# Earlier first scores, one more low part on GpSimd and a fixed GpSimd order in the second attention layer of a decoder trunk

## The chip, the cores and the metric

The kernel runs on 1 core of one Trainium2 chip, in one launch. The metric is device microseconds of one execution. The engines are named as the profile names them: PE (TensorE matmul), PEld (its weight load), DVE (VectorE), ACT (ScalarE), POOL (GpSimd), SP (SyncE, which here only issues transfers).

## The reference

The kernel computes a decoder trunk of two layers on 256 tokens of width 1024, all in float32. The part that matters here is the second layer's attention:

```python
N_HEADS, HEAD_DIM, N_KV_HEADS, WINDOW, D_FF = 16, 64, 4, 128, 2816
# layer 0: block-sparse attention with its own q, k, v; then a gated ConvFFN
# layer 1:
hk = rmsnorm(x, kv_norm); k, v = split(hk @ w_kv_b)          # shared K/V, 4 heads
q = partial_rope(heads(rmsnorm(x, attn_norm[1]) @ w_q_b))    # 16 heads
# sliding window of 128, each query head with a learned sink:
logits = q k^T / 8, masked to the band
m = max(max(logits), sink); e = exp(logits - m)
p = e / (sum(e) + exp(sink - m))
x = x + (p v) @ w_o_b
x = x + conv_ffn(rmsnorm(x, ffn_norm[1]))
return rmsnorm(x, final_norm)
```

## The kernel before, in words

**Products.** Each float32 matrix product is made of three matmuls in fp32r: high part by high part, high by low, low by high. So each operand is split: a high part `wh` or `hi` (a rounded copy, made by ACT) and a low part `wl` or `lo` (operand minus high part, made by DVE or POOL). A projection step of `proj` (L345 to L347) is one 128-row chunk of the contraction: three matmuls of 512 columns. A step of `Down.units` (L587 to L590) is six of them.

**Weights.** The weights come in units of 128 x 2048 numbers, in the order of use. `fetch(i)` lets SP issue the transfer of unit i into one of three `raw` buffers; `hi_part` (L181) and `lo_part` (L187 on POOL, L189 or L191 on DVE) make the two parts of a piece, in four `hi` and four `lo` buffers. `prepare(i)` puts a unit's pieces into a chain of steps: high, low, high, low; its last step makes the last low part and then fetches unit i + 3. Here U_QB to U_QB+3 are the q weights of layer 1, U_OB to U_OB+3 its output weights (one unit is two 128-row chunks, the first 1024 numbers and the second 1024), U_UP1 and following the up weights of its FFN. From U_OB+1 on a unit is cut into two pieces of 1024, apart from U_UP1+1 to +3. Before the change POOL makes the low parts of all of U_OB+2 and of the second half of U_OB+3, each 1024 numbers in two instructions of 512; DVE makes all others.

**The order written by the program.** `clock` is a plan's clock, in planned nanoseconds. Whatever is written for PE advances it by `tick`; `chain(key, (delay, step), ...)` puts off a step until the clock has passed its due time (each delay counts from the moment when the step before it was written). `require(key)` writes the pending steps of a key at once. A step of `proj` ticks 640, a step of `Down.units` 1280.

**Layer 1's attention.** There are four groups (g) of four heads, two pairs of heads (j = 2g, 2g + 1) each. `scores(g)` writes the score matmuls (L432 to L434 for the diagonal block of the first 128 queries, L439 for the second 128), `softmax` their chain: masking and row maximum on DVE (L457), exponentials on ACT (L468), a merge of two column blocks on POOL (L463), reciprocal on DVE (L473) and scaling on DVE (L480) and ACT (L478). POOL first writes the sink into the edge columns (L451). `probs_T(j)` transposes a pair's probabilities on PE (L493), which ACT (L502) and DVE (L499) copy; `values(g)` multiplies by v (L538), and ACT (L545) and DVE (L546) split the result o(g). Between these, `fill(ns)` draws steps from a generator until its budget is used up: first the 16 steps of the second half of q, `q_half(1)`, and then 12 steps of the output projection, units U_OB to U_OB+2 (D0 to D11 in the text). What `fill` draws too much is carried over as a negative budget. Ahead of `scores(0)` stands `fill(lead)`. For each half of q, `rotate` copies the projection on ACT (L1013), applies the rotary embedding on DVE (L374 to L380, the rotation), transposes on PE (L386) and splits on ACT (L397) and DVE (L392).

**The order in which engines run.** Within `tc.manual_schedule(engines=...)` an engine keeps the order in which the program wrote its instructions. Outside it, the order on each engine is a list made at compile time, in which an instruction that is ready goes ahead of an earlier one that is not. PE, ACT, DVE and SP are manual up to layer 0's attention (`manual`, closed at L551); in layer 1 only ACT is, from the last group's `values` on (`fixed`, L563, closed in `after_b`, L1044). In both cases each engine runs its list in order.

Of the kernel before, what the change touches and what calls it, by code (L numbers as in the profile page):

```python
# [54 lines left out]
U_OB = U_QB + 4  # L55
# [6 lines left out]
def trunk(ctx: ExitStack, tc, x, xw, pos, cpk, fin, w, out):  # L62
# [34 lines left out]
    def f(ap):  # L97
        return ap.bitcast(F32)
# [4 lines left out]
    def half(n):  # L103
        return slice(n * 512, (n + 1) * 512)
# [34 lines left out]
    def chain(key, *steps, urgent=0):  # L139

        def run(k):
            if urgent:
                with tc.high_priority(offset=urgent):
                    steps[k][1]()
            else:
                steps[k][1]()
            if k + 1 < len(steps):
                put_off.append((clock[0] + steps[k + 1][0], key, lambda: run(k + 1)))
        put_off.append((clock[0] + steps[0][0], key, lambda: run(0)))
# [16 lines left out]
    def fetch(i):  # L166
        if i < N_UNITS:
            raws[i] = wp.tile([P, UNIT], F32, tag="raw", name=f"wr{i}", bufs=3)
            for c in (slice(0, UNIT // 2), slice(UNIT // 2, UNIT)) if 2 <= i < 10 else (slice(0, UNIT),):
                nc.sync.dma_start(raws[i][:, c], w[i][:, c])  # L170

    def gain_of(i, c):

        if not U_KV <= i < U_OB:
            return None
        col = (G_KV + 4 * (i - U_KV) if i < U_QB else G_ATTN1 + 4 * ((i - U_QB) % 2)) + c.start // 512
        return cp[:, col:col + 1]

    def hi_part(i, c):
        g = gain_of(i, c)  # L180
        nc.scalar.activation(wq[i][0][:, c], raws[i][:, c], AF.Copy, **({} if g is None else {"scale": g}))  # L181

    def lo_part(i, c):
        g, raw, hi, lo = gain_of(i, c), raws[i][:, c], f(wq[i][0][:, c]), wq[i][1][:, c]
        if i == U_OB + 2 or i == U_OB + 3 and c.start:
            for h in (half(0), half(1)):
                nc.gpsimd.tensor_tensor(out=lo[:, h], in0=raw[:, h], in1=hi[:, h], op=ALU.subtract)  # L187
        elif g is None:
            nc.vector.tensor_tensor(out=lo, in0=raw, in1=hi, op=ALU.subtract)  # L189
        else:  # L190
            nc.vector.scalar_tensor_tensor(out=lo, in0=raw, scalar=g, in1=hi, op0=ALU.mult, op1=ALU.subtract)  # L191

    def weights(i):
        wq[i] = (spaced(wp, UNIT, F32R, "hi", f"wh{i}", 4),
                 spaced(wp, UNIT, F32R, "lo", f"wl{i}", 4))

    def prepare(i):

        if i >= N_UNITS:
            return  # L200
        n = 4 if i <= 5 or 1 <= i - U_UP0 <= 3 or 1 <= i - U_UP1 <= 3 or U_KV <= i <= U_OB else 2
        cut = [slice(k * UNIT // n, (k + 1) * UNIT // n) for k in range(n)]
        w_time[0] = max(clock[0] + 200.0, w_time[0] + 4500.0, 34000.0 if i == 7 else 0.0)

        def first():
            weights(i)
            hi_part(i, cut[0])

        def last():
            lo_part(i, cut[-1])  # L210
            fetch(i + 3)

        steps = [(w_time[0] - clock[0], first)]
        for k in range(n - 1):
            steps.append((2000.0 / n, lambda k=k: lo_part(i, cut[k])))
            steps.append((2000.0 / n, lambda k=k: hi_part(i, cut[k + 1])))
        chain(("w", i), *steps, (2000.0 / n, last))

    def used(i):

        prepare(i + 4)
# [184 lines left out]
    fixed = ExitStack()  # L406

    def attention(qk, ready, filler, lead, rate, msk, vcol, sink):
# [6 lines left out]
        def fill(ns):  # L415
            budget[0] += ns
            while budget[0] > 0:
                try:
                    budget[0] -= next(filler)
                except StopIteration:  # L420
                    return

        def scores(g):
            while g not in qk:
                next(filler)
            require("qk", g)
            qh, ql, kh_, kl_, kcol, diag = qk[g]
            sd, sa, sb = bank("t" if o_down[0].acc else "acc"), bank("u"), bank("u")
            for p in range(2):
                dh, dl = (t.rearrange("p (e t) -> p t e", e=2) for t in diag(p))  # L430
                o = pairs(sd[:, p * S:(p + 1) * S])
                nc.tensor.matmul(o, ql[:, p, blk(0)], dh, start=True, stop=False)  # L432
                nc.tensor.matmul(o, qh[:, p, blk(0)], dl, start=False, stop=False)
                nc.tensor.matmul(o, qh[:, p, blk(0)], dh, start=False, stop=True)  # L434
            for p in range(2):
                for k, (q_, k_) in enumerate(((ql, kh_), (qh, kl_), (qh, kh_))):
                    for e, o in ((1, sb), (0, sa)):
                        r = slice(e * HD, (e + 1) * HD)
                        nc.tensor.matmul(o[:, p * S:(p + 1) * S], q_[r, p, blk(1)], k_[r, kcol(p)],  # L439
                                         start=(k == 0), stop=(k == 2))  # L440
            tick(1600)
            return [softmax(2 * g + p, p, sd, (sa, sb)) for p in range(2)]
# [106 lines left out]
        ready(oT)  # L549
        fill(lead)  # L550
        manual.close()  # L551
        n_g = NH // 4
        state = scores(0)
        for g in range(n_g):
# [244 lines left out]
    def part(i, c):  # L799
        hi_part(i, c)  # L800
        lo_part(i, c)
# [105 lines left out]
    mask = one.tile([P, S], F32, name="mask")  # L907
# [11 lines left out]
    qk = {}  # L919
# [40 lines left out]
    def ready_a(oT):  # L960
        o_down.append(Down(U_OA, 4, oT, lambda i: require("o", i)))

    attention(qk, ready_a, filler_a(), 9200.0, lambda g: (7000.0, 3500.0, 2000.0) if g < 3 else (4500.0, 2000.0, 1500.0), mask, lambda h: h, False)
    nc.gpsimd.affine_select(out=mask[:, :P], in_=mask[:, :P], compare_op=ALU.is_gt, fill=NEG, base=0,
                            pattern=[[1, P]], channel_multiplier=-1)
# [43 lines left out]
    qk = {}  # L1009
# [5 lines left out]
    def q_half(a):  # L1015
        hi, lo = quad(), quad()
        u = U_QB + 2 * a
        for b in range(NB):
            o = bank("acc")
            yield from proj(o, xT, b, cols512(u), (u, u + 1) if b else ())  # L1020
            rotate(o, 4, b, hi, lo, ("qk", 2 * a), lambda t, b=b, o=o: q_out(t, b, o),
                   wait=750.0 if a or not b else 750.0, turn=2500.0 if a else 1000.0 if not b else 300.0)
        for g in (2 * a, 2 * a + 1):
            c = slice(2 * (g % 2), 2 * (g % 2) + 2)
            qk[g] = (hi[:, c], lo[:, c], kT[:, 0:2], kT[:, 2:4], lambda p, a=a: a, lambda p, a=a: diagonal(0)(a))
# [4 lines left out]
    def filler_b():  # L1030
        yield from q_half(1)
        yield from o_down[0].units(0, 3)

    def ready_b(oT):
        o_down.append(Down(U_OB, 4, oT, lambda i: require("o", i)))

    attention(qk, ready_b, filler_b(), 2100.0, lambda g: (2700.0, 1400.0, 1000.0) if g else (3300.0, 1700.0, 1000.0), mask, lambda h: 2 * (h // 8) + h % 2, True)

    hT = new_hT()
    y = [quad(F32, "y") for _ in range(2)]  # L1040
# [151 lines left out]
```

## Time and profile before

| | |
|---|---|
| Median of 3 runs | 547.96 us (547.95 to 548.14) |
| The profiled execution's own time | 547.73 us |
| Its span | 546.0 us, 9916 instructions |
| PE, PEld busy | 537.8 us (98%), 494.0 us (90%) |
| DVE, ACT, POOL busy | 418.4, 372.2, 132.2 us |
| Granted clock | 0.998 |
| Read from HBM | 99.30 MB, mean 184 GB/s |

Time is in microseconds from the span's start. The stages that the text names: layer 1's k, v and q projections end near 311, its attention lies between 311 and 358, the end of its output projection and the start of the FFN follow, the FFN fills 370 to 520, and the tail ends at 546. A row of the timeline gives start, length, engine, line, operation, tiles and shapes, count, and in brackets the idle time of the engine ahead of it with what ended that time. [...]

### The profile page before, as it was taken

The page shows a single profiled execution, that of the slowest core. Times are in us where ns is not written, and L with a number is a line of the kernel's source. Part 1 is how long each engine was busy: PE and PEld are TensorE (multiplying, and loading weights), DVE is VectorE, ACT ScalarE, POOL GpSimd, SP SyncE. Part 2 cuts the span into 40 slices and gives each one's busy share as a digit, 9 for nine tenths or more (in the row PEclk, how much of TensorE's full clock was granted, in tenths as well). Part 3 has the DMA queues.
Part 4 walks back from the last instruction along what each step waited for, and adds up shares of the span by engine and source line. Part 5 has one row for each costly group of instructions (what it writes and reads, how often), then busy time and mean ns, then how long its engine had stood idle before and what let it go on. Part 6 is the DMA issues. An engine that isn't in the chain of part 4 may idle for free.

```text
span 546.0 us, 9916 instructions
## 1 busy us (share of the span) xinstructions
PE 537.8 (98%) x3742; PEld 494.0 (90%) x3742; DVE 418.4 (77%) x869; ACT 372.2 (68%) x731; POOL 132.2 (24%) x164
## 2 busy tenths in 40 slices
PE   9999999999999999999999999999999999999995
PEld 7888888899999999988888877789999999998884
DVE  6798878689899888864467788889898888884414
ACT  6979777677677777744358798797567777663314
POOL 8422102016223233120001145202332332310003
PEclk9999999999999999999999999999999999999999
DMA  8974445342655665566553534242375656666301
GB/s 317 392 261 175 181 154 185 125 155 79 221 208 200 221 232 206 187 230 226 184 202 144 174 146 155 77 155 88 145 263 201 213 196 214 251 227 215 113 0 77
DMA packets 16464, 100.99 MB, mean 185 GB/s; under 512 B 1952, under 2 KB 2080, under 8 KB 5920
## 3 DMA queue, kind: packets, MB, share of 16 engines
q1 hardware_dynamic: 16128, 100.09, 51.2%
q8 instruction: 29, 0.48, 0.3%
q10 hardware_dynamic: 288, 0.26, 0.1%
q14 instruction: 19, 0.16, 0.1%
HBM read 99.30 MB, written 1.05 MB: 184 GB/s over the span
## 4 chain that ended last, share of the span: by engine, by line
PE 90%; ACT 5%; DVE 3%; issue 1%; DMA 1%; POOL 0%; DVEq 0%; ACTq 0%; POOLq 0%
PE acc L590 8%; PE acc L588 8%; PE acc L587 8%; PE u L681 7%; PE u L682 7%; PE u L680 6%; PE t L681 6%; PE t L682 6%; PE t L680 6%; PE acc L345 5%; PE acc L346 5%; PE acc L347 5%; PE acc L792 2%; PE acc L681 2%; PE acc L682 2%; PE acc L680 2%
## 5 line engine op out<-in xcount | busy, mean ns | idle before, releaser
L189 DVE TENSOR_TENSOR wl<-wr,wh 128x1024 fp32r<-128x1024 f32 (+1 forms) x187 | 204.2, 1112 | 50.3 <-ACT wh L181 49.7
L181 ACT ACTIVATE wh<-wr 128x1024 fp32r<-128x1024 f32 (+1 forms) x190 | 176.7, 958 | 51.4 <-PE acc L590 42.4
L726 POOL TENSOR_TENSOR m<-m,m 128x256 f32<-128x256 f32 x44 | 70.8, 1610 | 166.0 <-DVE m L721 84.2
L587 PE MATMUL acc<-wh,q 128*128 128x512 f32 x238 | 92.2, 387 | 0.2 <-ACT q L545 0.2
L588 PE MATMUL acc<-wl,q 128*128 128x512 f32 x238 | 90.6, 381 | 0.0
L680 PE MATMUL u<-q,wh 128*128 128x256 f32 x320 | 88.3, 277 | 0.0
L681 PE MATMUL u<-q,wh 128*128 128x256 f32 x320 | 88.2, 276 | 0.1
L682 PE MATMUL u<-q,wl 128*128 128x256 f32 x320 | 87.9, 275 | 0.0
L680 PE MATMUL t<-q,wh 128*128 128x256 f32 x288 | 79.2, 275 | 0.0
L681 PE MATMUL t<-q,wh 128*128 128x256 f32 x288 | 79.2, 275 | 0.0
L682 PE MATMUL t<-q,wl 128*128 128x256 f32 x288 | 79.2, 275 | 0.0
L590 PE MATMUL acc<-wh,q 128*128 128x512 f32 x238 | 74.9, 380 | 0.0
L681 PEld LDWEIGHTS u<-q,wh 128*128 128x128 f32 x320 | 61.4, 192 | 0.3 <-DVE q L309 0.3
L682 PEld LDWEIGHTS u<-q,wl 128*128 128x128 f32 x320 | 61.4, 192 | 0.0
L680 PEld LDWEIGHTS u<-q,wh 128*128 128x128 f32 x320 | 61.3, 192 | 0.0
L680 PEld LDWEIGHTS t<-q,wh 128*128 128x128 f32 x288 | 55.3, 192 | 0.0
L681 PEld LDWEIGHTS t<-q,wh 128*128 128x128 f32 x288 | 55.3, 192 | 0.0
L682 PEld LDWEIGHTS t<-q,wl 128*128 128x128 f32 x288 | 55.3, 192 | 0.0
L587 PEld LDWEIGHTS acc<-wh,q 128*128 128x128 f32 x238 | 45.0, 189 | 7.0 <-ACT q L545 0.6
L590 PEld LDWEIGHTS acc<-wh,q 128*128 128x128 f32 x238 | 44.8, 190 | 6.2 <-issue 0.2
L588 PEld LDWEIGHTS acc<-wl,q 128*128 128x128 f32 x238 | 45.1, 189 | 5.8 <-issue 0.2
L345 PE MATMUL acc<-wh,q 128*128 128x512 f32 x128 | 50.2, 392 | 0.0
(182 smaller groups left out, 1008.5 us busy)
## 6 DMA issues: line engine op xcount, KB each, us to landing
wr<-in_w SPq DMA_DIRECT2D x82, 1024.0 KB, 4.8
wr<-in_w SPq DMA_DIRECT2D x16, 512.0 KB, 6.5
first<-in_xw SPq DMA_DIRECT2D x7, 384.0 KB, 6.4
xr<-in_x SPq DMA_DIRECT2D x2, 512.0 KB, 8.3
fin_t<-in_fin SPq DMA_DIRECT2D x1, 512.0 KB, 5.6
out<-ot SPq DMA_DIRECT2D x1, 512.0 KB, 2.6
first<-in_xw SPq DMA_DIRECT2D x1, 388.0 KB, 3.5
out<-m ACTq DMA_DIRECT2D x1, 256.0 KB, 2.1
```

The costliest lines, as they stand in the source:

```text
L181: nc.scalar.activation(wq[i][0][:, c], raws[i][:, c], AF.Copy, **({} if g is None else {"scale": g}))
L189: nc.vector.tensor_tensor(out=lo, in0=raw, in1=hi, op=ALU.subtract)
L345: nc.tensor.matmul(o, xh[:, blk(b)], wh, start=(c == 0), stop=False)
L346: nc.tensor.matmul(o, xh[:, blk(b)], wl, start=False, stop=False)
L347: nc.tensor.matmul(o, xl[:, blk(b)], wh, start=False, stop=(c == KC - 1))
L587: nc.tensor.matmul(o, ph[:, blk(b)], turns(hi[:, s_]), start=first, stop=False)
L588: nc.tensor.matmul(o, ph[:, blk(b)], turns(lo[:, s_]), start=False, stop=False)
L590: nc.tensor.matmul(o, pl[:, blk(b)], turns(hi[:, s_]), start=False, stop=end)
L680: nc.tensor.matmul(o, hi[:, s_], xh, start=(c == 0), stop=False)
L681: nc.tensor.matmul(o, hi[:, s_], xl, start=False, stop=False)
L682: nc.tensor.matmul(o, lo[:, s_], xh, start=False, stop=(c == KC - 1))
L726: nc.gpsimd.tensor_tensor(out=h, in0=gs, in1=t[1], op=ALU.mult)
```

## The change

It has four parts. The `lead` of layer 1's attention is 1500 instead of 2100. The second half of unit U_OB+1 has its low part made by POOL instead of DVE. The delay of a unit's last step (last low part and fetch) is set for three units: 300 for U_OB+1, 2500 for U_OB+2 and U_OB+3, where it was 1000. From the first scores of layer 1 until `after_b`, POOL is manual too. The diff, whole:

```diff
     def lo_part(i, c):
         g, raw, hi, lo = gain_of(i, c), raws[i][:, c], f(wq[i][0][:, c]), wq[i][1][:, c]
-        if i == U_OB + 2 or i == U_OB + 3 and c.start:
+        if i == U_OB + 2 or i in (U_OB + 1, U_OB + 3) and c.start:
             for h in (half(0), half(1)):
                 nc.gpsimd.tensor_tensor(out=lo[:, h], in0=raw[:, h], in1=hi[:, h], op=ALU.subtract)
         elif g is None:
@@
         for k in range(n - 1):
             steps.append((2000.0 / n, lambda k=k: lo_part(i, cut[k])))
             steps.append((2000.0 / n, lambda k=k: hi_part(i, cut[k + 1])))
-        chain(("w", i), *steps, (2000.0 / n, last))
+        late = {U_OB + 1: 300.0, U_OB + 2: 2500.0, U_OB + 3: 2500.0}.get(i, 2000.0 / n)
+        chain(("w", i), *steps, (late, last))
@@
         ready(oT)
         fill(lead)
         manual.close()
+        if sink:
+            fixed.enter_context(tc.manual_schedule(engines={mybir.EngineType.Pool}))
         n_g = NH // 4
         state = scores(0)
@@
-    attention(qk, ready_b, filler_b(), 2100.0, lambda g: ..., mask, ..., True)
+    attention(qk, ready_b, filler_b(), 1500.0, lambda g: ..., mask, ..., True)
```

`sink` is true only for layer 1.

More of the change, by code (lines that the diff above doesn't have):

```diff
@@ L1035, in ready_b @@
         o_down.append(Down(U_OB, 4, oT, lambda i: require("o", i)))
-    attention(qk, ready_b, filler_b(), 2100.0, lambda g: (2700.0, 1400.0, 1000.0) if g else (3300.0, 1700.0, 1000.0), mask, lambda h: 2 * (h // 8) + h % 2, True)
+    attention(qk, ready_b, filler_b(), 1500.0, lambda g: (2700.0, 1400.0, 1000.0) if g else (3300.0, 1700.0, 1000.0), mask, lambda h: 2 * (h // 8) + h % 2, True)
     hT = new_hT()
```

## The prediction

> **What bounds the kernel now.** I read the page's first part, then the busy time by stage, then PE's timeline through layer 1's attention, and last what ACT, DVE and POOL did ahead of each hole.
>
> ```profile
> PE 537.8 (98%) x3742; PEld 494.0 (90%) x3742; DVE 418.4 (77%) x869; ACT 372.2 (68%) x731; POOL 132.2 (24%) x164
> ```
>
> PE is the bound almost everywhere. The stages (columns: us, then each engine's busy time and instructions, clock, DMA):
>
> ```profile
> 370.00:520.00 150.00, 150.00 (x1185) 145.38 (x1184) 118.00 (x183) 97.24 (x152) 35.52 (x23) 1.00 0.56 194
> 520.00:546.00 26.00, 19.92 (x99) 17.42 (x97) 8.06 (x19) 7.47 (x17) 4.37 (x4) 0.96 0.10 40
> ```
>
> ```profile
> 308.00:323.00 15.00, 14.83 (x86) 12.32 (x85) 12.60 (x41) 13.20 (x33) 2.39 (x7) 1.00 0.46 176
> 323.00:345.00 22.00, 21.72 (x150) 17.15 (x148) 19.04 (x65) 19.03 (x56) 13.08 (x19) 1.00 0.27 96
> 345.00:358.00 13.00, 12.78 (x88) 10.05 (x88) 9.58 (x34) 9.05 (x30) 2.02 (x4) 1.00 0.23 83
> ```
>
> The second FFN (370 to 520) leaves PE no idle time, and the change ends before it. Layer 1's attention, 308 to 358, shows 0.17 + 0.28 + 0.22 us idle. A matmul's shown length overlaps the next one's, so the holes are larger than that; I take them from starts. The change can win only there, or lose there.
>
> ```profile
> 315.35 0.38 PE L345 MATMUL acc<-wh,q 128*128 128x512 f32 x1
> 315.90 0.98 PE L439 MATMUL u<-q,q 64*128 64x256 f32 x12 [0.17 <-DVE q L392]
> ...
> 323.58 0.28 PE L434 MATMUL acc<-kd,q 128*128 128x256 f32 x1
> 323.78 0.97 PE L439 MATMUL u<-q,q 64*128 64x256 f32 x12
> ...
> 330.09 0.46 PE L587 MATMUL acc<-wh,q 128*128 128x512 f32 x1
> 330.39 0.38 PE L588 MATMUL acc<-wl,q 128*128 128x512 f32 x1
> 330.61 0.38 PE L587 MATMUL acc<-wh,q 128*128 128x512 f32 x1
> 330.82 0.38 PE L588 MATMUL acc<-wl,q 128*128 128x512 f32 x1
> 331.30 0.62 PE L493 MATMUL u<-ident,m 128*128 128x128 f32 x3
> 331.68 0.68 PE L590 MATMUL acc<-wh,q 128*128 128x512 f32 x2
> ...
> 338.48 0.70 PE L590 MATMUL acc<-wh,q 128*128 128x512 f32 x2
> 339.36 0.48 PE L587 MATMUL acc<-wh,q 128*128 128x512 f32 x1 [0.18 <-ACT q L545]
> ...
> 341.73 0.49 PE L493 MATMUL u<-ident,m 128*128 128x128 f32 x3
> 341.98 0.68 PE L590 MATMUL acc<-wh,q 128*128 128x512 f32 x2
> ...
> 350.11 0.46 PE L587 MATMUL acc<-wh,q 128*128 128x512 f32 x1
> 350.79 0.62 PE L493 MATMUL u<-ident,m 128*128 128x128 f32 x3 [0.22 <-ACT m L478]
> 351.16 0.46 PE L588 MATMUL acc<-wl,q 128*128 128x512 f32 x1
> ```
>
> A 512-column product takes 0.215 us of PE (330.61 to 330.82), so a `proj` step of three is 0.65 and a `Down` step of six 1.29. The holes:
> - S1, first scores: 315.57 to 315.90, 0.33; a change to 64-row tiles costs 0.09 anyway (323.58 + 0.11 to 323.78), so about 0.23.
> - S2, transposes of pair 2: 331.04 to 331.30, 0.26, and three of them take 0.38 against 0.25 at 341.73: 0.39.
> - S3, `Down` unit 1 waits for o(1): the second L590 began at 338.80 (its end, 339.18, less 0.38), so 339.02 to 339.36: 0.34.
> - S4, transposes of pair 6: 0.68 from 350.11, where 0.30 is usual after a transpose (330.09 to 330.39): 0.38, and 0.37 against 0.25: 0.50.
>
> Together 1.46 us, all that can be won but crumbs of 0.1.
>
> **The change part by part.**
>
> *Lead 2100 to 1500.* A step costs 640 on the plan's clock: 2100 is used up after 4 steps (-460 left), 1500 after 3 (-420). The next budgets, 3300, 1700 and 1000, still draw 5, 3 and 1, so scores 0 stand behind 3 steps instead of 4 and scores 1 behind 12 instead of 13. Nothing is removed; three products go behind. What fed the scores before:
>
> ```profile
> 311.79 2.00 ACT L181 ACTIVATE wh<-wr 128x1024 fp32r<-128x1024 f32 x2
> 314.23 0.61 ACT L397 ACTIVATE q<-t 128x512 fp32r<-128x512 f32 x1 [0.44 <-PE t L386]
> ```
>
> ```profile
> 312.52 0.29 DVE L380 TENSOR_TENSOR m<-rb 128x128 f32<-128x128 f32 x1
> 312.88 2.36 DVE L189 TENSOR_TENSOR wl<-wr,wh 128x1024 fp32r<-128x1024 f32 x2
> 315.16 0.68 DVE L392 TENSOR_TENSOR q<-t,q 128x512 fp32r<-128x512 f32 x1
> ```
>
> ```profile
> 313.59 0.60 PE L386 MATMUL t<-ident,m 128*128 128x128 f32 x4
> ```
>
> The rotation ended at 312.81 and PE turned q only at 313.59, behind twelve products. With nine it can at 312.94, 0.65 earlier. ACT is in L181 to 313.79, so L397 runs 313.79 to 314.40, not 314.23 to 314.84.
>
> *The low part of U_OB+1.* L392 waited for DVE's second L189, whose end is about 315.24. That instruction (half of 2.36, 1.18 us) leaves DVE: free at about 314.06, it starts L392 at 314.40 and ends at 315.08, and L439 can begin 0.75 us earlier. The program emits the two parts of the scores (L434, L439) together, yet the trace has a product of L345 right ahead of L439: PE's order here is a compiled list order that puts in what is ready. I take all of S1, 0.23; bounds: 0 if the order keeps the old distance, 0.33 with the shape change too. POOL pays, by these rows (and has time, idle 16.50 us):
>
> ```profile
> 318.59 0.88 POOL L463 TENSOR_TENSOR m<-m 128x128 f32<-128x128 f32 x2 [16.50 <-ACT m L468]
> ...
> 323.83 5.03 POOL L187 TENSOR_TENSOR wl<-wr,wh 128x512 fp32r<-128x512 f32 x4 [0.61 <-ACT wh L181]
> ```
>
> Two of L187 are 2 x 1.26 = 2.52 us, 314.0 to 316.5, and merges begin near 318: nothing on the path. SP's fetch of U_UP1 waits for it, some 1.3 us later than 315.24; ACT takes up those weights only at 339.70:
>
> ```profile
> 339.70 1.04 ACT L181 ACTIVATE wh<-wr 128x1024 fp32r<-128x1024 f32 x1
> ```
>
> So more than 20 us cover it; without that cover it would cost its 1.3.
>
> *`late` and the given order on POOL.* On the plan's clock, from the end of the first q half: U_OB+1 is due at 1700 and written at 1920; its first low part (due 2920) is written at 3960, after the scores' tick of 1600, its second high part (due 4960) at 5240, so the last step is due at 5540 (with 1000: 6240). The first exponentials are written at 5240 too, their merge due 600 later, 5840. So POOL's order is: four L451, the pair for U_OB+1, the four merges of group 0, four L451, the first pair of U_OB+2, the merges of group 1 (three due at 15480, the fourth 16760), the second pair (due 18020), L451 for group 2, the pair of U_OB+3, merges. Before, all four L187 of U_OB+2 stood in one block ahead of group 1's merges, which came late:
>
> ```profile
> 326.99 0.51 ACT L468 ACTIVATE m<-m,hst 128x257 f32<-128x257 f32 x1
> ```
>
> ```profile
> 328.79 1.72 POOL L463 TENSOR_TENSOR m<-m 128x128 f32<-128x128 f32 x4
> ...
> 341.31 1.01 POOL L463 TENSOR_TENSOR m<-m 128x128 f32<-128x128 f32 x1 [0.98 <-ACT m L468]
> ```
>
> An exponential of group 1 that a merge needs ended at 327.50, and POOL came at 328.79. With only one pair ahead (323.8 to 326.4) that 1.3 us goes, more than S2's 0.39: I take all of it; bounds 0 (norms late for ACT's sake) to 0.39. The fetch of U_UP1+1 goes behind the second pair, to about 331.5 instead of 328.9: 8 us ahead of even U_UP1's use, which comes before its own. That of U_UP1+2 keeps its place behind the pair of U_OB+3.
>
> *Later fills.* A `Down` step costs 1280. Before, 2700 drew the last three q steps and D0 ahead of pair 2, then came D1, pair 3, D2, scores 2, D3 and D4, pair 4, D5, pair 5, D6, scores 3. Now 2700 draws the last four q steps (-40 left), 1400 draws D0 and D1 (-1200), 1000 draws none, and so on: pair 2, D0, D1, pair 3, scores 2, D2, D3, pair 4, D4, D5, pair 5, scores 3. So D2 and D3 stand behind values(1), 1.29 us more between it and D4, which must wait for o(1): S3's 0.34 goes (bounds 0, 0.34). Scores 2 lose D2 as a cover; D1 before them and D2, values(1) and D3 behind can be drawn ahead, at no cost if the list order does it. S4 gets nothing directly: two steps stand between values(2) and pair 6 as before. I leave it (bounds 0, 0.50, if its scores get DVE sooner).
>
> The tail (520 to 546) has 6 us without PE, but runs the same instructions after 150 us of full PE: no change there. Sum: 0.23 + 0.39 + 0.34 = 0.96 us. The profiled execution took 547.73 (span 546.0 and 1.7 around it), so 546.8; the median stands 0.23 above it, so 547.0.
>
> **The rivals.** *All four holes close* (S4 too): -1.46, 546.5. For it: scores 3 come right behind pair 5, so DVE's masking may start earlier. Against: S4 ends by ACT's L478, and ACT loses no work.
>
> *The second pair of U_OB+2 collides with the rotation* (slower). It now follows group 1's merges, near 329, where DVE rotates q's second half:
>
> ```profile
> 340.77 1.23 DVE L189 TENSOR_TENSOR wl<-wr,wh 128x1024 fp32r<-128x1024 f32 x1
> ```
>
> ```profile
> 330.52 0.28 DVE L374 TENSOR_TENSOR rb<-m,cs 128x128 f32<-128x128 f32 x1
> ...
> 331.10 0.29 DVE L380 TENSOR_TENSOR m<-rb 128x128 f32<-128x128 f32 x1
> ```
>
> The merge at 341.31 took 1.01 us, 0.5 over the pair's 0.44 each at 318.59, and ended 0.32 after this L189: POOL waited for DVE. If DVE waits likewise, L187 can hold the rotation up to 2 x 1.26 = 2.5 us, and through it L386, L397, L392 and scores 2. It decides once the pair starts before L380 ends. Less a cover of up to D2's 1.29 it costs 1.2, on PE's fixed order 2.5; S2 and S3 would not pay for it: 547.96 - 0.23 + 1.2 to 2.5 = 548.9 to 550.2. Against: the masking, which reads PSUM and one SBUF tile, took 0.48 us outside the block of L187 and inside it:
>
> ```profile
> 317.32 0.48 DVE L457 CUSTOM_DVE_ANT_0 m<-u,mask,nsink 128x256 f32<-128x256 f32 x1
> ...
> 325.31 0.48 DVE L457 CUSTOM_DVE_ANT_0 m<-u,mask,nsink 128x256 f32<-128x256 f32 x1
> ```
>
> The rotation reads SBUF twice, though, as L189 does.
>
> [...]
>
> *Little moves*: the list order had already put products where they fit, and gives holes back elsewhere; 0 to -0.5, 547.7.
>
> **How the numbers follow.** Forecast (-0.5 to -1.1) 0.38; all holes (beyond -1.1) 0.34; little (within 0.5 either way) 0.16; collision 0.12, 0.11 of it beyond +1.1. 0.2% is 1.1 us, about what a measurement can tell. So faster 0.34, same 0.55, slower 0.11. Range 546.1 (all 1.46 and 0.4 of crumbs) to 549.0 (lower end of the collision); the forecast's own is 546.8 to 547.5.
>
> **What would show it.** Right: L386 near 312.9 and L439 near 315.1 with no hole; two L187 ahead of POOL's first merge; merges of group 1 from about 326.5; no wait of L587 on L545 after values(1); the first L680 of FFN 1 about 1 us earlier. Wrong: a stretched L374 or L480 beside L187, a wait of L439 on L392 at scores 2, or holes that only move behind 339.

## The result and the profile after

The kernel became slower: 552.73 us (median of 5 runs, 552.36 to 553.03) against 547.99 (547.95 to 548.34), a ratio of 1.0083 (95% interval 1.0072 to 1.0094). The prediction was 547.0, with a range of 546.1 to 549.0: the time lies above the range, and on the other side of the kernel before. The profiled execution took 552.73 us, of which the span is 551.0.

The page's first part shows almost nothing: the same 3742 products, and 2.4 us more of "busy" on PE. The last line of the fence, out of the page's second part, does show something. Each figure there is a slice of 13.8 us, and the 25th (331 to 344) has a granted clock below 0.9:

```profile
span 551.0 us, 9935 instructions
...
PE 540.2 (98%) x3742; PEld 495.9 (90%) x3742; DVE 420.3 (76%) x868; ACT 372.7 (68%) x731; POOL 132.2 (24%) x166
...
PEclk9999999999999999999999998999999999999999
```

Busy time by stage of the changed kernel (columns as before: PE, PEld, DVE, ACT, POOL, clock, DMA):

```profile
308.00:323.00 15.00, 14.96 (x88) 12.27 (x88) 12.05 (x40) 13.20 (x34) 4.83 (x10) 1.00 0.52 187
323.00:345.00 22.00, 18.90 (x123) 14.36 (x123) 17.65 (x56) 15.42 (x49) 12.03 (x17) 0.92 0.27 96
...
375.00:525.00 150.00, 150.00 (x1185) 145.38 (x1184) 118.03 (x184) 97.09 (x152) 35.49 (x23) 1.00 0.54 194
```

The loss is in one stretch, 323 to 345: PE is without work for 3.10 us there, where it was 0.28, and runs at a clock of 0.92. The waits of PE between 308 and 372 (what waited, for what, total, times, longest) name the place:

```profile
PE t L387 <- DVE m L381: 2.9, 1, 2.9
PE t L539 <- DVE pT L500: 0.3, 1, 0.3
PE u L494 <- ACT m L479: 0.2, 1, 0.2
```

L387 is the transpose of q's second half (L386 before; the code has moved down by a line there), and L381 the last instruction of the rotation (L380 before). PE's timeline of the changed kernel, first at the scores 0 and at pair 2, then around L387:

```profile
315.23 0.38 PE L346 MATMUL acc<-wh,q 128*128 128x512 f32 x1
315.55 0.97 PE L440 MATMUL u<-q,q 64*128 64x256 f32 x12
...
329.14 0.46 PE L590 MATMUL acc<-wh,q 128*128 128x512 f32 x1
329.80 0.62 PE L494 MATMUL u<-ident,m 128*128 128x128 f32 x3 [0.19 <-ACT m L479]
...
333.53 0.38 PE L590 MATMUL acc<-wh,q 128*128 128x512 f32 x1
333.75 0.38 PE L591 MATMUL acc<-wl,q 128*128 128x512 f32 x1
337.03 0.66 PE L387 MATMUL t<-ident,m 128*128 128x128 f32 x4 [2.91 <-DVE m L381]
337.63 0.58 PE L433 MATMUL t<-kd,q 128*128 128x256 f32 x1
...
339.93 0.63 PE L590 MATMUL acc<-wh,q 128*128 128x512 f32 x1
340.36 0.63 PE L591 MATMUL acc<-wl,q 128*128 128x512 f32 x1
...
341.88 1.52 PE L539 MATMUL t<-pT,v 128*64 128x256 f32 x16
```

Read two things. From L591 to L387 there is a hole: 337.03 less 333.965 (333.75 and 0.215 of pace) is 3.06 us. And behind it two successive products of 512 columns stand 0.43 apart (339.93 to 340.36), twice the 0.215 of 333.53 to 333.75. PE runs there at half its pace.

What DVE did meanwhile, and what POOL did:

```profile
331.32 2.21 DVE L189 TENSOR_TENSOR wl<-wr,wh 128x1024 fp32r<-128x1024 f32 x1 [1.25 <-ACT wh L181]
333.46 0.68 DVE L500 TENSOR_TENSOR pT<-u,v 128x512 f32<-128x512 f32 x1
334.06 1.25 DVE L375 TENSOR_TENSOR rb<-m,cs 128x128 f32<-128x128 f32 x1
335.24 1.42 DVE L380 TENSOR_TENSOR rb<-m,sn 128x64 f32<-128x64 f32 x2
336.69 0.29 DVE L381 TENSOR_TENSOR m<-rb 128x128 f32<-128x128 f32 x1
```

```profile
314.42 2.56 POOL L187 TENSOR_TENSOR wl<-wr,wh 128x512 fp32r<-128x512 f32 x2 [11.84 <-ACT wh L181]
...
326.80 0.95 POOL L464 TENSOR_TENSOR m<-m 128x128 f32<-128x128 f32 x2 [0.16 <-ACT m L469]
...
329.94 2.51 POOL L187 TENSOR_TENSOR wl<-wr,wh 128x512 fp32r<-128x512 f32 x2
332.40 1.55 POOL L452 COPY m<-nsink 128x2 f32<-128x2 f32 x4
333.91 2.52 POOL L187 TENSOR_TENSOR wl<-wr,wh 128x512 fp32r<-128x512 f32 x2
```

From 331.32 to 336.98 DVE shows no idle time, only instructions that have become long. One half low part, L189, takes 2.21 us instead of 1.22; the first rotation instruction 1.25 instead of 0.28; the next two 1.42 instead of 0.35. That is 0.99 + 0.97 + 1.07 = 3.03 us more. Each long one is let go about where one of POOL's L187 ends. The pair at 329.94 (second half of U_OB+2) ends at 332.45, and L189 ends 1.08 us behind that, within its usual 1.22; the two of the pair at 333.91 (U_OB+3) end at 335.17 and 336.43, where L375 and L380 are released.

In the kernel before, the order on DVE was another. The rotation stood ahead of L189, and PE came to the transposes later than the rotation was done:

```profile
331.31 1.22 DVE L189 TENSOR_TENSOR wl<-wr,wh 128x1024 fp32r<-128x1024 f32 x1
332.44 0.68 DVE L499 TENSOR_TENSOR pT<-u,v 128x512 f32<-128x512 f32 x1
```

```profile
333.93 0.60 PE L386 MATMUL t<-ident,m 128*128 128x128 f32 x4
```

Its rotation (quoted in the prediction) ended at 331.39, so it had 2.54 us to spare before PE asked at 333.93. In the changed kernel L189 and L500 are listed ahead of it, and nothing is left to spare. ACT's list changed likewise: the copy of the projection, which the rotation reads, stood ahead of ACT's high part (L181, 329.90) in the kernel before and stands behind it (L181, 330.23) in the changed one. The row of before, then that of the changed kernel:

```profile
329.33 0.67 ACT L1013 ACTIVATE m<-acc,rstd 128x512 f32<-128x512 f32 x1
```

```profile
331.18 0.68 ACT L1016 ACTIVATE m<-acc,rstd 128x512 f32<-128x512 f32 x1
```

So the rotation could not have begun before 331.86, wherever DVE had it. The chain of the changed kernel (start, length, what) shows the whole path, from the weights on ACT to the matmuls that run slow:

```profile
330.33 0.97 ACT wh L181
...
331.32 2.21 DVE wl L189
...
335.31 1.35 DVE rb L380 x2
...
337.03 0.66 PE t L387 x4
```

Before any experiment this makes one theory: two pairs of POOL's L187 meet DVE's low part and rotation (3 us), and PE's clock falls after so long a hole (the rest). The rivals: the given order on POOL itself costs (small work waits behind large), or the new list order costs, with the L187 as bystanders. The expectations below call the first half of the theory "port", after a guess of the author's (two readers of SBUF take turns); no trace shows a port, only how long the instructions took.

### The profile page after: what moved, and what is told of

Read it like the earlier page. It is cut to its first block, busy times and chain, and to the rows that moved or that the text cites. A ratio compares the mean times of both kernels' runs of the same rounds, so it can differ in the third digit from the quotient of the medians.

```text
span 551.0 us, 9935 instructions
## 1 busy us (share of the span) xinstructions
PE 540.2 (98%) x3742; PEld 495.9 (90%) x3742; DVE 420.3 (76%) x868; ACT 372.7 (68%) x731; POOL 132.2 (24%) x166
## 3 DMA queue, kind: packets, MB, share of 16 engines
HBM read 99.30 MB, written 1.05 MB: 182 GB/s over the span
## 4 chain that ended last, share of the span: by engine, by line
PE 90%; DVE 4%; ACT 3%; issue 1%; DMA 1%; DVEq 0%; ACTq 0%
PE acc L593 8%; PE acc L591 8%; PE acc L590 8%; PE u L684 7%; PE u L685 6%; PE u L683 6%; PE t L685 6%; PE t L683 6%; PE t L684 6%; PE acc L346 5%; PE acc L347 5%; PE acc L348 5%; PE acc L795 2%; PE acc L684 2%; PE acc L685 2%; PE acc L683 2%
## 5 line engine op out<-in xcount | busy, mean ns | idle before, releaser
L189 DVE TENSOR_TENSOR wl<-wr,wh 128x1024 fp32r<-128x1024 f32 (+1 forms) x186 | 203.3, 1113 | 50.9 <-ACT wh L181 50.6
L181 ACT ACTIVATE wh<-wr 128x1024 fp32r<-128x1024 f32 (+1 forms) x190 | 176.3, 956 | 50.9 <-PE acc L593 42.2
L729 POOL TENSOR_TENSOR m<-m,m 128x256 f32<-128x256 f32 x44 | 69.2, 1573 | 167.7 <-DVE m L724 97.9
L591 PE MATMUL acc<-wl,q 128*128 128x512 f32 x238 | 91.0, 382 | 0.0
L591 PEld LDWEIGHTS acc<-wl,q 128*128 128x128 f32 x238 | 45.2, 190 | 6.1 <-issue 0.3
```

The costliest lines, as they stand in the source:

```text
L591: nc.tensor.matmul(o, ph[:, blk(b)], turns(lo[:, s_]), start=False, stop=False)
L729: nc.gpsimd.tensor_tensor(out=h, in0=gs, in1=t[1], op=ALU.mult)
```

## The experiments

Each ratio is against runs of the kernel before on the same chip. One measure from the traces stands beside it: the distance from ACT's second copy of q's first half (L1013 before, L1016 in the changed kernel), just ahead of what the change touches, to the first product of the FFN, just behind:

| kernel | copy, first product | distance | against before | ratio (95%) |
|---|---|---|---|---|
| before | 311.20, 363.69 | 52.49 | | |
| after | 311.69, 368.70 | 57.01 | +4.52 | 1.0083 (1.0072 to 1.0094) |
| a_lead | 311.15, 364.74 | 53.59 | +1.10 | 1.002 (1.001 to 1.003) |
| b_order | 311.16, 365.50 | 54.34 | +1.85 | 1.0034 (1.0021 to 1.0047) |
| c_no_order | 311.34, 364.88 | 53.54 | +1.05 | 1.0017 (1.0008 to 1.0027) |
| e_writes | 311.17, 363.63 | 52.46 | -0.03 | 1.0002 (0.9992 to 1.0011) |
| m_first | 311.68, 365.05 | 53.37 | +0.88 | 1.0023 (1.0013 to 1.0034) |
| n_second | 311.47, 364.88 | 53.41 | +0.92 | 1.0013 (1.0004 to 1.0023) |
| f_fill | 311.66, 368.37 | 56.71 | +4.22 | 1.0084 (1.007 to 1.0098) |
| k_part | 311.91, 363.94 | 52.03 | -0.46 | 0.9994 (0.9985 to 1.0002) |
| p_lead2100 | 311.48, 366.05 | 54.57 | +2.08 | 1.0031 (1.0019 to 1.0044) |
| s_b_edges | 311.50, 364.16 | 52.66 | +0.17 | 1.0003 (0.9993 to 1.0012) |
| q_edges | 311.43, 364.61 | 53.18 | +0.69 | 1.001 (1.0001 to 1.0019) |
| r_edges_late | 311.71, 364.16 | 52.45 | -0.04 | 0.9997 (0.9988 to 1.0006) |

In the changed kernel all stands 0.49 us later already at that copy, ahead of the change. The copies of the other kernels scatter as far, from 311.15 to 311.91, and why was not tried. It is in the 552.73, and not in the 4.52.

**The lead alone** (the kernel before, with one number changed):

```diff
-    attention(qk, ready_b, filler_b(), 2100.0, ...
+    attention(qk, ready_b, filler_b(), 1500.0, ...
```

> Only the lead is changed (1500 for 2100); POOL's order and its low parts are as before. PE's and DVE's lists are then nearly those of the changed kernel: on DVE the rotation of q's second half stands behind a low part (L189) and a copy (L499) instead of ahead of them. Theory (port): the pair of L187 for U_OB+3 starts near 333.4 and meets the rotation, which waits for one or both: a hole of PE of 1 to 2 us ahead of scores 2, 549 to 551. Rival (lost cover: `Down` step D2 no longer stands ahead of scores 2): the hole comes from PE's list, so it is as large as in the changed kernel, 552 to 553, with DVE's instructions at their usual lengths.

Slower by 1.10 us on the table's measure. The wait of PE, the only large one, and the DVE row behind it, both from this kernel:

```profile
PE t L386 <- DVE m L380: 0.8, 1, 0.8
```

```profile
333.67 1.24 DVE L380 TENSOR_TENSOR m<-rb 128x128 f32<-128x128 f32 x1
```

The shorter lead alone already puts the rotation so late in DVE's list that its last instruction meets the pair of U_OB+3 on POOL, and takes 1.24 us instead of 0.29. The "lead" is no tuning of the front: it renumbers everything behind.

**The given order on POOL alone** (the kernel before, with the added `manual_schedule`):

```diff
+        if sink:
+            fixed.enter_context(tc.manual_schedule(engines={mybir.EngineType.Pool}))
```

> Only POOL's given order; lead, low parts and late steps as before. PE's and DVE's lists are word for word those of before, and POOL's has the four L187 of U_OB+2 ahead of group 1's merges as before. Theory (port): 547.7 to 548.3. Rival (a given order on POOL costs by itself, because it waits in line): over 549.

Slower by 1.85 us, where the theory expected next to nothing; the rival is right for this kernel. The mechanism is another one. The first row is POOL's, the last one ACT's:

```profile
323.78 2.53 POOL L187 TENSOR_TENSOR wl<-wr,wh 128x512 fp32r<-128x512 f32 x2 [1.73 <-ACT wh L181]
326.24 0.56 POOL L451 COPY m<-nsink 128x2 f32<-128x2 f32 x4
```

```profile
326.47 0.41 ACT L468 ACTIVATE m<-m,hst 128x129 f32<-128x129 f32 x1 [1.54 <-POOL m L451]
```

Group 1's four edge copies, 0.56 us in all, are written behind the first pair, and ACT's exponentials wait for the edge columns. With the old lead this holds; with the new one the edges of group 1 come out ahead of that pair (in the changed kernel L452 runs at 320.70, L187 at 324.11), so this cost is not in the 4.52.

**The changed kernel without the given order:**

```diff
-        if sink:
-            fixed.enter_context(tc.manual_schedule(engines={mybir.EngineType.Pool}))
```

> The changed kernel without POOL's given order. PE's and DVE's lists are word for word those of the changed kernel; on POOL all four L187 of U_OB+2 stand ahead of group 1's merges again, so only the pair of U_OB+3 can meet the rotation. Theory (port): L189 beside it falls from 2.21 to 1.2 us, the rotation meets one or two L187 instead of queueing behind three, a hole of 1 to 2 us, 549 to 551. Rival (PE's list, lost cover): unchanged, 552 to 553.

1.05 us instead of 4.52. PE and DVE run the same lists as in the changed kernel; only POOL's order differs, and with it one meeting is left, that of the pair of U_OB+3 with the rotation's last instruction:

```profile
331.22 1.23 DVE L189 TENSOR_TENSOR wl<-wr,wh 128x1024 fp32r<-128x1024 f32 x1 [1.34 <-ACT wh L181]
...
333.55 1.25 DVE L381 TENSOR_TENSOR m<-rb 128x128 f32<-128x128 f32 x1
```

So the lists of PE and DVE by themselves do not cost the 4.5. What they cost with no L187 beside the rotation, the next run shows.

**The two pairs without their reading.** POOL's second pair of U_OB+2 and the pair of U_OB+3 become writes (two `memset` of the same tile, 1.97 us instead of 2.51). Those low parts are left out of the output. The lists of PE and DVE stay those of the changed kernel.

```diff
+            if i > U_OB + 1 and c.start:
+                for _ in range(2):
+                    nc.gpsimd.memset(f(lo), 0.0)
+                return
```

> The changed kernel with the last two pairs of L187 (second half of U_OB+2, U_OB+3) replaced on POOL by memsets of the same tiles, two for each half: POOL stays busy at the same places of its list but reads no SBUF; the low parts of these halves are left out (zero). PE's and DVE's lists are unchanged. Theory (port: two readers of SBUF take turns): L189, L375 and L380 go back to 1.2, 0.3 and 0.35 us, the rotation ends near 334, the hole of 3.1 us and the low clock behind it vanish: 546.5 to 548. Rival 1 (PE's list): 552 to 553. Rival 2 (DVE waits for POOL by order, not for its port): as long as the memsets are busy, 550 to 552.

The loss is gone: -0.03 us. POOL still works all through the rotation, as its row and then DVE's show (lines are 5 further down here):

```profile
332.39 1.96 POOL L189 MEMSET wl<- 128x1024 f32 x2
```

```profile
329.19 1.27 DVE L486 TENSOR_SCALAR m<-m,hst 128x128 f32<-128x128 f32 x1
...
332.56 0.28 DVE L380 TENSOR_TENSOR rb<-m,cs 128x128 f32<-128x128 f32 x1
332.75 0.35 DVE L385 TENSOR_TENSOR rb<-m,sn 128x64 f32<-128x64 f32 x2
333.14 0.29 DVE L386 TENSOR_TENSOR m<-rb 128x128 f32<-128x128 f32 x1
```

So here it is POOL's reading of SBUF (of two inputs; one was not tried) that holds these two-input instructions of DVE, not POOL's being busy: beside reads the first took 1.25 us and the next two 1.42, beside writes 0.28 and 0.35. The rotation ends at 333.43 and PE takes up the transposes at 333.49, without a hole: the changed order leaves the rotation no slack (0.06 us, against 2.54 before), but costs nothing by itself. And with the collisions gone nothing is gained either; that is the other half of the wrong forecast.

**One pair at a time.** m_first replaces only the second pair of U_OB+2, n_second only the pair of U_OB+3 (low parts left out likewise).

```diff
+            if i == U_OB + 2 and c.start:      # n_second: i == U_OB + 3
+                for _ in range(2):
+                    nc.gpsimd.memset(f(lo), 0.0)
+                return
```

> The changed kernel with only the second pair of U_OB+2 as memsets (that low part is left out, zero); the pair of U_OB+3 stays. PE's and DVE's lists unchanged. Theory (port, and a clock that falls only after a long hole): L189 back to 1.2 us, L381 or one L380 still waits for an L187, a hole near 1 us as without the given order, no low clock: 548.8 to 549.6.

> The changed kernel with only the pair of U_OB+3 as memsets (left out, zero); the second pair of U_OB+2 stays. Theory: L189 takes 2.2 us, the rotation its usual 0.3 and ends near 335, a hole near 1 us, clock 1.00: 548.8 to 549.8. So the two pairs alone cost about 1 each, together 4.5, the difference being the second wait in a row and the low clock. Rival (costs add up without a clock effect): the two alone sum to 4.5, one of them at least 2.2 above before, over 550.4.

Either pair alone costs 0.9 us (0.88, 0.92). PE's row of m_first, then that of n_second:

```profile
334.95 0.66 PE L391 MATMUL t<-ident,m 128*128 128x128 f32 x4 [0.82 <-DVE m L385]
```

```profile
334.77 0.66 PE L391 MATMUL t<-ident,m 128*128 128x128 f32 x4 [0.87 <-DVE m L385]
```

Together they cost 4.5, not 1.8. First, with the first pair alive, the rotation begins 1 us later, and the second pair takes two of its instructions instead of one: three waits, 3.03 us. Second, the clock. From the transposes to values(1), the same list of instructions took 4.85 us in the changed kernel (337.03 to 341.88) and 3.24 in m_first (334.95 to 338.19), 3.24 in n_second, 3.23 in e_writes: 1.61 us more. A window of 3.4 us behind the hole in the changed kernel, and the same window in m_first:

```profile
337.60:341.00 3.40, 3.40 (x13) 2.54 (x12) 1.87 (x9) 1.71 (x7) 0.00 (x0) 0.51 0.74 294
```

```profile
337.60:341.00 3.40, 3.40 (x34) 2.42 (x31) 3.15 (x16) 3.40 (x16) 0.87 (x2) 1.00 0.72 299
```

A hole of 1.0 us, 0.82 of it shown as idle, leaves the clock at 1.00; one of 3.06 us, 2.91 shown idle, is followed by a clock of 0.51 for 3.4 us. 3.06 + 1.61 = 4.67. The whole distance to e_writes, which has neither, is 4.55 (57.01 less 52.46), so these two terms account for it to within 0.12 us.

**The hole filled with other work.** To keep PE busy and see the clock stay, pair 3's transposes run seven times over (24 more of them, the output unchanged).

```diff
-                    nc.tensor.transpose(tp[:, e, k], ...
+                    for _ in range(7 if j == 3 else 1):
+                        nc.tensor.transpose(tp[:, e, k], ...
```

> The changed kernel with the eight-fold... transposes of pair 3 written seven times (24 more transposes, 2.6 us more work for PE, same results) so that PE is busy in most of the hole ahead of scores 2. Theory (the hole of 3.1 us itself brings the clock down to a half for 3 us): the granted clock stays at 1.00 behind it, and although PE does 2.6 us more, the time falls by about 1.5 us to 551.0 to 551.6. Rival (the low clock has another cause): clock low all the same, 552.5 or more.

```profile
332.63 3.22 PE L495 MATMUL t<-ident,m 128*128 128x128 f32 x28
337.02 0.66 PE L387 MATMUL t<-ident,m 128*128 128x128 f32 x4 [1.17 <-DVE m L381]
```

```profile
337.00:341.00 4.00, 3.98 (x38) 3.41 (x40) 2.90 (x13) 1.78 (x8) 0.00 (x0) 1.00 0.74 266
```

The hole stood at the same place, its idle part cut to 1.17 us, and the clock stayed at 1.00. The time did not fall with it (+4.22), because the compiled list put other products elsewhere. Counted from the copy of the table, values(1) begins 1.81 us earlier than in the changed kernel (340.04 and 341.88 on the two clocks), but with four products of 512 columns (0.86 us) fewer done ahead of it, and pairs 4 and 6 then wait anew (0.44 and 0.15 us shown idle). So it agrees with a clock that falls with PE's own idleness, as POOL and DVE met here as before; but that the time falls with the hole, as was expected, it did not show. The 1.61 us of clock rest on the comparison with m_first, n_second and e_writes.

**U_OB+1's low part alone** (the kernel before, with `lo_part`'s new condition only):

```diff
-        if i == U_OB + 2 or i == U_OB + 3 and c.start:
+        if i == U_OB + 2 or i in (U_OB + 1, U_OB + 3) and c.start:
```

> The kernel before with only the low part of U_OB+1's second half on POOL; lead, late steps and POOL's order as before. DVE's list keeps the rotation of q's second half ahead of L189, so no L187 meets it. Theory: L392 of the first scores no longer waits for L189, S1 shrinks by about 0.2 us, the rest as before: 547.5 to 548.0, at best a little faster. Rival (any more work on POOL costs): 548.5 or more.

547.54 against 548.11, ratio 0.9994 (0.9985 to 1.0002): at best half a microsecond, not told from none. Of all kernels it alone has a distance shorter by more than a tenth of a microsecond.

**The old lead, all else as changed**, and three kernels around the edge copies. p_lead2100 is the changed kernel with a lead of 2100. In s_b_edges (from b_order), q_edges (from p_lead2100) and r_edges_late (from q_edges) the edge copies are written ahead of the scores; r_edges_late also gives U_OB+2 and U_OB+3 their old delay.

```diff
         # s_b_edges, q_edges, r_edges_late: in scores(g), ahead of its tick
+            pre = [edges(2 * g + p) for p in range(2)] if sink else [None] * 2
         # r_edges_late
-        late = {U_OB + 1: 300.0, U_OB + 2: 2500.0, U_OB + 3: 2500.0}.get(i, 2000.0 / n)
+        late = {U_OB + 1: 300.0}.get(i, 2000.0 / n)
```

> The changed kernel with the lead back at 2100 (given order on POOL, low part of U_OB+1 and late steps stay). PE's and DVE's lists are then those of before but for U_OB+1: the rotation stands ahead of L189 and ends about 2.5 us before PE wants it. On POOL the edge copies of group 1 (L452) now stand behind the first pair of U_OB+2, as in the run with the given order alone, and the second pair ahead of group 1's fourth merge. Theory (the lead took the slack that would hide a collision; edges behind a pair cost 1 to 2 us by themselves): no hole ahead of the transposes of q, clock 1.00, 549 to 550.5. Rival (the collision costs the same with any lead): 552 or more.

> The given order on POOL alone, but the edge copies are written ahead of the scores' tick, so that group 1's stand ahead of the first pair of U_OB+2. PE's and DVE's lists as before. Theory (the given order cost 1.8 us because the exponentials of group 1 waited for edges queued behind a pair of L187): back to 547.8 to 548.5. Rival (merges or other things behind one another in the given order): still 549 or more.

> The changed kernel with the lead at 2100 and the edge copies written ahead of the scores' tick. Only the second pair of U_OB+2 (behind three merges of group 1) and that of U_OB+3 can now hurt. Theory: the second pair meets the rotation near 330 to 331 or L189, but 2.5 us of slack hide it; the fourth merge waits for the pair, so pair 3's transposes come late: 547.3 to 549. Rival: the collision costs its 2 to 3 us again, 550 or more.

> As the last one, with the late steps of U_OB+2 and U_OB+3 back at 1000: on POOL all four L187 of U_OB+2 stand ahead of group 1's merges as before, the edges ahead of them. Of the change there are left the low part of U_OB+1 on POOL (late 300) and the given order. Theory: the same as with the low part alone, 547.3 to 548.0, which is as fast as or a little faster than before. Rival (a given order costs something in itself): 548.5 or more.

p_lead2100 costs 2.08: the lead cannot be the sole cause. Here the edges wait behind the first pair as in b_order, and the second pair, at 330.55, meets the norm instead of the rotation (DVE's row):

```profile
330.40 2.73 DVE L481 TENSOR_SCALAR m<-m,hst 128x128 f32<-128x128 f32 x3
```

Three of these take 0.68 in b_order (330.54), with one merge on POOL beside their start, and 1.28 in the kernel before (328.90), beside POOL's merges all along. s_b_edges brings b_order's 1.85 down to 0.17, so the edges behind the pair were its cause. q_edges, with the edges early, still pays 0.69, with the same long norm (2.75 us). r_edges_late, whose second pair keeps the old delay, costs nothing (-0.04). A given order on POOL is free here, then, when the small work that others wait for goes first, and the large work is due where DVE has nothing urgent. It gains nothing either: no version here beats the kernel before beyond its interval.

## Why the prediction was wrong, by its steps

- **S1 was right, and small.** L440 begins at 315.55 with about 0.1 of hole; from q's copy it is 3.86 us against 4.70, of which 0.65 is the moved step and 0.19 gained (0.23 predicted). The pair for U_OB+1 runs at 314.42, ahead of the first merge, as said.
- **S2 was wrong.** Group 1's merges did come earlier (326.80 instead of 328.79), but pair 2's transposes still waited, for ACT's share of the norm: 0.19 idle before them at 329.80, the last line of the waits above. The chain of the kernel before had run there too: ACT's copy (329.33), its L181 (329.90) and its share of the norm (330.85) stand ahead of the transposes at 331.30, and no merge does. The term took all of the bound where its own lower end, "norms late for ACT's sake", was the truth.
- **S3 went, S4 went, and both came back.** No `Down` product waits for L546 any more, but values(2) now waits for a copy of the probabilities (L539 on L500, 0.3 in the waits above). In e_writes, with no collision, this wait and pair 2's remain, and the distance is that of before. The forecast of -0.96 added up holes; the list order made others. That was the rival "little moves", at a chance of 0.16.
- **"D1 before them and D2, values(1) and D3 behind can be drawn ahead, at no cost if the list order does it"** is the step that failed. It looked at what PE's list could draw ahead and not at what the lists of the engines that feed it would do. On ACT the rotation's input went behind L181, on DVE the rotation went behind L189 and L500, and its slack fell from 2.54 us to 0.06. The shorter lead alone did this (a_lead), and cost 1.10. The condition "if" was priced at nothing, and no row was named that covered it.
- **The collision was the right mechanism at the right place, mis-sized.** It was priced at 1.2 to 2.5 us with a chance of 0.12; it cost 4.5. Three terms were missing. L189 of U_OB+3 met the second pair of U_OB+2 as well, and U_OB+3's own pair came next: three waits of about 1 us, where one pair's length was taken as the most. D2, taken as a cover of 1.29, was not there, since PE's list had the transposes right behind D1's L591. And the hole of 3.06 us took the clock, another 1.61. The prediction's own sign of being wrong, a stretched L374, is the 1.25 us of L375.
- **The argument against the collision was of the wrong kind.** The masking kept its 0.48 us beside L187, but it reads PSUM and one SBUF tile; the rotation's instructions read two SBUF tiles, as the prediction itself noted. The prediction's own row of a merge held beside L189 (1.01 us at 341.31) had POOL as the loser; in the changed kernel it is DVE, with 1.25 us for L375 instead of 0.28. Beside POOL's writes (e_writes) the rotation kept its 0.28 and 0.35.
- **The clock was in no term.** In the changed kernel a hole with 2.91 us idle was followed by a clock of 0.51 for 3.4 us; holes with 0.82 (m_first), 0.87 (n_second) and 1.17 us idle (f_fill) left it at 1.00. What a hole between 1.17 and 2.91 does was not shown. The prediction's own collision of up to 2.5 us came near enough to this to deserve a sentence, and had none, though its row of the tail has a clock of 0.96 where 6.08 of 26 us are without PE.

## What to carry to other kernels

Before work that reads SBUF moves to GpSimd, or to a later place on it, look among DVE's instructions of that stretch for those with two SBUF inputs on PE's path: here L189, L375 and the two of L380 lost 0.99, 0.97 and 1.07 us beside GpSimd instructions of 1.26. The scaling (TENSOR_SCALAR) belongs on that list too: three of them took 2.73 us beside a pair (p_lead2100) and 0.68 in b_order. A number at the front of a planned order changes every list behind it, so a step that "can be drawn ahead" needs its slack read on every engine that feeds it, not on the bound one alone. And a hole's price is not always its length: the one of 3.06 us here cost 1.61, half as much again, in clock.

## What the runs showed of the hardware

- A DVE instruction of 0.28 us with two SBUF inputs took 1.25 beside a POOL subtraction of 1.26 us; four such instructions within 5.7 us (L189, a low part, L375 and the two of L380) took 3.03 us more together. Beside a POOL `memset` of 0.98 us the same instructions kept 0.28 and 0.35 us.
- Beside a `memset` another form took longer: the scaling (TENSOR_SCALAR, 128x128) at 329.19 in e_writes took 1.27 us, and so did the one at 329.69 in m_first, where the changed kernel has 0.38 at the same place. The one in e_writes began 0.23 us ahead of the `memset` of 329.42 and ended at 330.46.
- PE's granted clock fell to 0.5 only about 0.6 us after PE had resumed (the first product after the four transposes, 337.63, is the first at half pace) and stayed there for 3.4 us: it was 1.00 over 337.0 to 337.5, 0.51 over 337.6 to 341.0, and 1.00 again over 341.2 to 342.0.
